# A build-time order planner: a shared port for VectorE and GpSimd, and a lower planned cost for running sums

## The chip, the cores and the metric

The kernel runs on one core of a Trainium2 chip. Its time is the device time of one execution in microseconds (us); a lower one is better. Five engines matter: TensorE (PE in the profile; its weight loads are PEld), VectorE (DVE), ScalarE (ACT), GpSimd (POOL) and SyncE (SP), which issues the DMAs.

## The reference

Two layers (`DEPTH` 2) work on 512 latent tokens and 256 context tokens of width 1024. A layer normalizes and modulates its input, projects it once, runs three mixers beside each other, multiplies each by a gate, merges them and adds the result to the residual. The last layer computes outputs for the latent tokens alone.

```python
shift, scale, gate = jnp.split(sc @ w_mod + b_mod, 3, axis=-1)
h = rms_norm(x, norm_g) * (1 + scale[:, None]) + shift[:, None]
aq, ak, av, az, bq, bk, bv, bo, bz, bg, cq, ck, cv, cz, gm = split_proj(h @ w_in)
...
y_a = diff_head_norm(o_a, da_g, lam_init) * jax.nn.silu(az)
...
y_b = mlstm_out(h_b, bo, bz, ml_g)
...
y_c = o_c.reshape(B, S, BR_W) * jax.nn.silu(cz)

x = x + gate[:, None] * merge_branches((y_a, y_b, y_c), gm, w_br, w_out)
```

A is differential attention (two softmaxes per head, the second subtracted), B a bidirectional linear recurrence whose decays come from the gate columns `bg`, and C neighbourhood attention (32 columns of keys around each block of 16 query columns, and the context).

## The kernel before, in words

**The work of TensorE.** Its main stream is one long list of projections: for each of branch C, A and B the values (`proj_v`), keys, queries and gates of two heads or pairs at a time, then the merge gates and the branch projections (`wbr`), then the output projection (`wout`). All these matmuls write tiles named `pj`, of which two exist. Weights come by DMA in half tiles `wr`; ScalarE rounds each to its high half and GpSimd subtracts that from the original for the low half, both into a tile `wh`, of which four exist (`Stream.lower`; 409 of the 416 low halves are GpSimd's). Three matmuls multiply high by high, high by low and low by high.

**Side tasks** fill in between: for branch C scores `gp<-qk`, a row minimum (`m`), a biased copy with minimum (`p<-gp,cb,m`), exponentials, a normalization (`smc`, `p<-p,smc`), transposes `gp<-ident,p`, their copies `pt`, and the product with the values `gp<-pt,cb` and `gp<-pt,v`; for A the same in a single score tile `sc`, with minima `mna`; for B products with running sums. Three tasks have a fixed place: the **gates chain** (`branch_b_gates`), some twenty VectorE steps over 112 x 768 elements in one `v` and one `pt` tile, ending in copies `pt<-v` and twelve column transposes `gp<-ident,pt`; **`norm_rows`**, which transposes sums of squares (`gp<-ident,p`), takes the inverse root on 128 x 2 or 128 x 4 elements (`rr`, `rt`), and spreads it by `gp<-p,ones`; and **`make_h`**, which makes the projection's input `h` from it, two VectorE instructions and one of ScalarE for each of eight tiles and each segment (latents, context). In the merge of layer 0 `mod_rows` computes the rest of the modulation: 112 sums over 128 x 512 elements on VectorE, two inputs in SBUF (`cb`), the products dumped into the PSUM tile `sc`.

**What sets the order.** Nothing is reordered on the chip: a planner, `Sched`, runs while the program is built. `Timed` gives each instruction a cost from its size, and `run` adds it to the planned clock of its engine, `T`, not before the planned ends of what it reads and writes (`ready`). Each side task is a generator with its own planned time; between main matmuls, `slot` lets those run whose planned time has come. So a cost decides where an instruction stands in its engine's queue, and the chip then executes each queue in that order. `need` holds the main stream until a buffer is planned to be free, and the order of the side tasks goes on meanwhile: there are two `v` tiles, so the next `proj_v` needs the one that the gates chain holds, until that chain's last copies.

```python
    def need(self, tag):
        while not self._take(tag, self.T["P"]):
            self.idle()
```

Every recorded compute instruction carries the line of `Timed`'s last call, L344 before, so the names of the tiles tell groups apart; matmuls are L379 (`mm`), transposes L383 (`tr`), DMAs L331.

Of the kernel before, what the change touches and what calls it, by code (L numbers as in the profile page):

```python
# [19 lines left out]
PSUM = bass.MemoryType.PSUM  # L20
DRAM = bass.MemoryType.DRAM

D = 1024
# [64 lines left out]
class Chain:  # L88


    def __init__(self, gen, t, eng="P"):
        self.gen, self.t, self.eng, self.want, self.landed = gen, t, eng, None, 0.0
# [13 lines left out]
class Sched:  # L106
# [14 lines left out]
    def __init__(self, free):  # L121
        self.free = {t: [0.0] * n for t, n in free.items()}
        self.token = {}
        self.T = dict(P=0.0, D=0.0, A=0.0, G=0.0, S=0.0, Q=0.0, H=0.0)
        self.main = self.cur = Chain(None, 0.0)
        self.high, self.mid, self.side, self.hooks = [], [], [], []
        self.pe = 0.0
        self.seen = {}

    @staticmethod  # L130
    def span(ap):
# [31 lines left out]
    def run(self, eng, cost, reads, writes):  # L163
        c = self.cur
        start = max(self.T[eng], self.ready(eng, reads, writes))
        end = self.T[eng] = start + cost
        self.note(eng, reads, writes, end)
        c.settle()
        c.t, c.eng = end, eng
        if eng == "P" and c is not self.main:  # L170
            self.pe += cost
# [125 lines left out]
def _space(ap):  # L297
    return getattr(ap, "space", None)


def _elems(ap):
    n = 1
    for s in list(ap.shape)[1:]:
        n *= int(s)
    return n


class Timed:
# [5 lines left out]
    def __getattr__(self, name):  # L314
        f = getattr(self.real, name)

        def call(*args, **kw):
            aps = [v for v in list(args) + list(kw.values()) if hasattr(v, "shape")]
            n = max(_elems(v) for v in aps)
            small = sum(1 for v in aps if _elems(v) == 1 and n > 1)  # L320
            psum = any(_space(v) == PSUM for v in aps[1:] + aps[:1])
            writes = [kw["out"] if "out" in kw else args[0]]
            if "accum_out" in kw:
                writes.append(kw["accum_out"])
            if name == "tensor_tensor_reduce":
                writes.append(args[-1])
            reads = [v for v in aps if not any(v is w for w in writes)]
            if name == "dma_start":
                out = kw["out"]
                self.sched.dma(int(out.shape[0]), int(out.shape[0]) * _elems(out) * 4, reads, writes)  # L330
                return f(*args, **kw)  # L331
            if self.eng == "D":
                one = len([v for v in aps if _elems(v) == n]) <= 2 and name in ("tensor_copy", "tensor_scalar", "memset")
                cost = n / (1.92 if one and not psum else 0.96) + 69.0 + 61.0 * small
                if name == "reciprocal":
                    cost = 69.0 + 8.0 * n
                if name == "tensor_tensor_reduce":
                    cost += 220.0
            elif self.eng == "A":
                cost = n * 0.8333 + (51.0 if psum else 93.0) + 93.0 * small  # L340
            else:
                cost = n * 2.15 + 130.0
            self.sched.run(self.eng, cost, reads, writes)
            return f(*args, **kw)  # L344
        return call
# [1594 lines left out]
```

## Time and profile before

| what | value |
|---|---|
| time, median of 3 runs | 1974.73 us (1974.41 to 1976.49) |
| profiled execution: time | 1975.63 us |
| profiled execution: span | 1973.9 us |
| mean granted clock of TensorE | 0.984 |
| PE busy | 1865.8 us (95%) |
| DVE busy | 1363.2 us (69%) |
| ACT busy | 862.1 us (44%) |
| POOL busy | 617.3 us (31%) |

The span runs from the first to the last recorded instruction; the execution's time lies 1.7 us above it. "Idle before" a group is time in which its engine waited, with the engine and tile that released it. [...] Busy times of VectorE and GpSimd hold whatever an instruction waits for after it began.

### The profile page before, as it was taken

Reading aid. Unit: us, or ns where it says so; the run is one execution under the profiler, and the core shown is the slowest. Engines: PE = TensorE matmul, PEld = TensorE weight load, DVE = VectorE, ACT = ScalarE, POOL = GpSimd, SP = SyncE. Lnnn points to the kernel's source line nnn. Section 1 sums busy time; section 2 is a strip of 40 time slices with the busy share of each in tenths; the row PEclk is TensorE's granted clock in tenths of the full one; section 3 lists DMA queues with packets and bytes.
Section 4 is the critical chain, followed back from the end, with each engine's and each line's share of the span. In section 5 each row is a group of like instructions: output and inputs, shape, how many; then the busy total and the mean of one; then the engine's idle time right before and its main releaser. Section 6 shows DMA issues by size and latency. Waiting matters only on the chain.

```text
span 1973.9 us, 31993 instructions
## 1 busy us (share of the span) xinstructions
PE 1865.8 (95%) x11420; PEld 1636.1 (83%) x11420; DVE 1363.2 (69%) x3165; ACT 862.1 (44%) x1972; POOL 617.3 (31%) x498
## 2 busy tenths in 40 slices
PE   5989999999999999999999898999999999999997
PEld 2879998988889888888887777898979787888886
DVE  6587775888787877687835768676887777743336
ACT  4345544555544553222223444555555444433343
POOL 1242322121222222333334533424222323334454
PEclk9989999999999999999999999999999999999998
DMA  8233323222211122566645423333231212335554
GB/s 316 72 96 102 96 79 97 61 82 65 68 51 51 44 83 76 182 227 200 214 152 169 147 78 111 119 94 109 69 105 54 65 50 69 97 109 186 168 167 124
DMA packets 137247, 222.26 MB, mean 113 GB/s; under 512 B 15984, under 2 KB 47776, under 8 KB 137088
## 3 DMA queue, kind: packets, MB, share of 16 engines
q1 hardware_dynamic: 137088, 220.22, 35.6%
q8 instruction: 91, 1.49, 0.3%
q14 instruction: 68, 0.56, 0.1%
HBM read 177.36 MB, written 28.11 MB: 104 GB/s over the span
## 4 chain that ended last, share of the span: by engine, by line
PE 47%; issue 21%; DVE 17%; POOL 9%; ACT 3%; DMA 2%; SPq 0%; POOLq 0%; DVEq 0%; ACTq 0%
PE pj L379 34%; POOL wh L344 8%; PE gp L379 7%; PE gp L383 3%; DVE p L344 3%; PE sc L379 3%; DVE qk L344 2%; DVE pt L344 2%; DVE t L344 1%; DMA cb<-in_wmodr_dram 1%; DVE v L344 1%; DVE sc L344 1%; ACT wh L344 1%; DVE h L344 1%; ACT p L344 1%
## 5 line engine op out<-in xcount | busy, mean ns | idle before, releaser
L379 PE MATMUL pj<-h,wh 128*128 128x512 f32 (+1 forms) x5664 | 1124.4, 351 | 20.1 <-DVE gz L344 9.9
L379 PEld LDWEIGHTS pj<-h,wh 128*128 128x128 f32 x5664 | 897.3, 191 | 144.0 <-DVE gz L344 10.3
L344 POOL TENSOR_TENSOR wh<-wr,wh 128x512 fp32r<-128x512 f32 x409 | 558.9, 1372 | 1269.4 <-ACT wh L344 1250.8
L344 ACT CAST wh<-wr 128x512 fp32r<-128x512 f32 x416 | 256.9, 620 | 395.5 <-PE pj L379 193.4
L379 PE MATMUL pj<-wh,h 128*128 128x256 f32 x1728 | 239.3, 289 | 4.1 <-DVE h L344 2.5
L379 PEld LDWEIGHTS pj<-wh,h 128*128 128x128 f32 x1728 | 219.7, 193 | 7.1 <-DVE h L344 3.7
L344 DVE TENSOR_TENSOR pt<-gp,pt 128x512 fp32r<-128x512 f32 (+1 forms) x224 | 123.6, 572 | 80.2 <-ACT pt L344 79.2
L344 ACT CAST pt<-gp 128x512 fp32r<-128x512 f32 (+1 forms) x224 | 105.1, 497 | 155.6 <-PE gp L383 155.1
L379 PE MATMUL pj<-v,wh 128*128 128x512 f32 (+1 forms) x576 | 161.6, 357 | 6.5 <-DVE t L344 6.2
L383 PE MATMUL gp<-ident,p 128*128 128x128 f32 x720 | 110.3, 278 | 23.4 <-DVE p L344 15.5
L379 PEld LDWEIGHTS pj<-v,wh 128*128 128x128 f32 x576 | 103.5, 189 | 23.9 <-DVE t L344 7.9
L379 PE MATMUL gp<-pt,v 128*128 128x256 f32 x864 | 120.2, 287 | 0.0
L383 PEld LDWEIGHTS gp<-ident,p 128*128 128x128 f32 x720 | 84.0, 142 | 40.4 <-issue 18.1
L379 PEld LDWEIGHTS gp<-pt,v 128*128 128x128 f32 x864 | 113.0, 195 | 2.0
L344 ACT ACTIVATE t<-pj 128x512 f32<-128x512 f32 (+1 forms) x118 | 63.4, 538 | 99.7 <-PE pj L379 93.5
L379 PE MATMUL pj<-qk,wh 128*128 128x512 f32 (+1 forms) x288 | 102.2, 355 | 0.0
L344 DVE TENSOR_REDUCE mna<-sc 128x1 f32<-128x768 f32 (+1 forms) x80 | 67.8, 847 | 38.5 <-PE sc L379 38.3
L344 DVE SCALAR_TENSOR_TENSOR t<-t,pj 128x512 f32<-128x512 f32 x66 | 38.8, 594 | 73.2 <-PE pj L379 71.2
L344 ACT ACTIVATE p<-sc,mna 128x768 f32<-128x768 f32 (+1 forms) x80 | 65.5, 819 | 53.7 <-DVE mna L344 53.5
L379 PE MATMUL sc<-qk 128*128 128x512 f32 (+1 forms) x360 | 82.0, 336 | 5.0 <-ACT p L344 4.9
L344 DVE CUSTOM_DVE_ANT_0 sc<-cb,prm 128x512 f32<-128x512 f32 x56 | 60.0, 1072 | 25.4 <-DMA cb<-in_wmodr_dram 24.1
L344 DVE TENSOR_TENSOR qk<-t,qk 64x768 fp32r<-64x768 f32 (+1 forms) x64 | 64.0, 1000 | 14.2 <-ACT qk L344 11.8
(157 smaller groups left out, 2208.8 us busy)
## 6 DMA issues: line engine op xcount, KB each, us to landing
wr<-in_wu_dram SPq DMA_DIRECT2D x304, 256.0 KB, 2.9
cb<-in_wmodr_dram SPq DMA_DIRECT2D x64, 256.0 KB, 3.4
wr<-in_wout_dram SPq DMA_DIRECT2D x64, 256.0 KB, 2.8
wr<-in_wbr_dram SPq DMA_DIRECT2D x48, 256.0 KB, 2.9
q<-qk SPq DMA_DIRECT2D x160, 64.0 KB, 2.4
cb<-vd SPq DMA_DIRECT2D x32, 256.0 KB, 3.2
qk<-in_xT_dram SPq DMA_DIRECT2D x16, 384.0 KB, 5.0
pd<-t SPq DMA_DIRECT2D x16, 384.0 KB, 3.9
```

Of the source, the lines that this page charges most:

```text
L344: return f(*args, **kw)
L379: PE.matmul(o, l, r, start=start, stop=stop)
L383: PE.transpose(o, i, idn)
```

## The change

`Sched` remembers the last eight planned intervals of GpSimd and of those VectorE instructions that neither read nor write PSUM. A GpSimd instruction, or such a VectorE instruction, whose planned start falls into an interval of the other engine is planned to start at that interval's end. Besides, the planned cost of `tensor_tensor_reduce` (the running sums and minima) loses the 220 ns that were added to its length. Nothing else changes: every engine gets the same instructions, the same number of each, in another order. The lines of the later file lie nine further down (L353, L388, L392).

```diff
@@ -126,6 +126,15 @@
         self.high, self.mid, self.side, self.hooks = [], [], [], []
         self.pe = 0.0
         self.seen = {}
+        self.port = {"D": deque(maxlen=8), "G": deque(maxlen=8)}
+
+    def shared(self, eng, start, cost):
+
+        for a, b in self.port["G" if eng == "D" else "D"]:
+            if a <= start < b:
+                start = b
+        self.port[eng].append((start, start + cost))
+        return start
 
     @staticmethod
     def span(ap):
@@ -163,6 +172,8 @@
     def run(self, eng, cost, reads, writes):
         c = self.cur
         start = max(self.T[eng], self.ready(eng, reads, writes))
+        if eng == "G" or eng == "D" and not any(_space(v) == PSUM for v in list(reads) + list(writes)):
+            start = self.shared(eng, start, cost)
         end = self.T[eng] = start + cost
         self.note(eng, reads, writes, end)
         c.settle()
@@ -334,8 +345,6 @@
                 cost = n / (1.92 if one and not psum else 0.96) + 69.0 + 61.0 * small
                 if name == "reciprocal":
                     cost = 69.0 + 8.0 * n
-                if name == "tensor_tensor_reduce":
-                    cost += 220.0
             elif self.eng == "A":
                 cost = n * 0.8333 + (51.0 if psum else 93.0) + 93.0 * small
             else:
```

Three places where the order moved. First TensorE in branch C of layer 0, where the gates chain's twelve column transposes `gp<-ident,pt` stand among the main stream (`pj`). Before:

```order
L379 MATMUL pj<-h,wh 128x256 x24
L383 MATMUL gp<-ident,pt 128x112 x2
L379 MATMUL pj<-h,wh 128x512 x3
L383 MATMUL gp<-ident,pt 128x112 x2
L379 MATMUL pj<-h,wh 128x512 x3
L383 MATMUL gp<-ident,pt 128x112 x8
```
After:

```order
L388 MATMUL pj<-h,wh 128x512 x24
L388 MATMUL gp<-pt,cb 128x256 x6
L388 MATMUL gp<-pt,v 128x256 x6
L388 MATMUL pj<-h,wh 128x256 x6
L392 MATMUL gp<-ident,p 128x128 x8
L388 MATMUL pj<-h,wh 128x256 x18
L388 MATMUL pj<-wh,h 128x256 x6
L392 MATMUL gp<-ident,pt 128x112 x2
L388 MATMUL pj<-wh,h 128x256 x6
L392 MATMUL gp<-ident,pt 128x112 x4
L388 MATMUL pj<-wh,h 128x256 x6
L392 MATMUL gp<-ident,pt 128x112 x6
```
Before, the first two transposes stand right ahead of the gate projection's 24 matmuls of 512 columns and the other ten among these. After, the first two follow all 24 of them, the 24 of 256 columns behind these (6 and 18) and six matmuls of the next `proj_v` (`pj<-wh,h`).

Second, TensorE in branch C of layer 1, from the last gate projection of the first pairs (`pj<-h,wh`) on; `proj_v` of the other pairs is `pj<-wh,h`, and it needs the `v` tile that the gates chain holds. Before:

```order
L379 MATMUL gp<-qk 128x256 x2
L379 MATMUL gp<-qk,q_12892 128x256 x2
L379 MATMUL pj<-wh,h 128x256 x6
L383 MATMUL gp<-ident,pt 128x112 x4
L379 MATMUL pj<-wh,h 128x256 x6
L383 MATMUL gp<-ident,pt 128x112 x2
L379 MATMUL pj<-wh,h 128x256 x18
L383 MATMUL gp<-ident,pt 128x112 x2
L379 MATMUL pj<-wh,h 128x256 x12
L383 MATMUL gp<-ident,pt 128x112 x4
L379 MATMUL gp<-qk 128x256 x2
L379 MATMUL gp<-qk,q_12944 128x256 x2
```
After:

```order
L388 MATMUL pj<-h,wh 128x512 x3
L388 MATMUL gp<-qk 128x256 x2
L388 MATMUL gp<-qk,q_12908 128x256 x2
L388 MATMUL gp<-qk 128x256 x2
L388 MATMUL gp<-qk,q_12954 128x256 x2
L388 MATMUL gp<-pt,cb 128x256 x6
L388 MATMUL gp<-pt,v 128x256 x6
L392 MATMUL gp<-ident,p 128x128 x8
L388 MATMUL gp<-qk 128x256 x2
L388 MATMUL gp<-qk,q_12954 128x256 x2
L388 MATMUL gp<-qk 128x256 x2
L388 MATMUL gp<-qk,q_13068 128x256 x2
```
Before, the next `proj_v` follows the score groups of one block and goes on between transposes. After, no main matmul stands in the 28 rows that begin with the second one here: four rounds of two score groups, `gp<-pt,cb`, `gp<-pt,v` and eight transposes, before `pj<-wh,h` begins.

At the same place VectorE, the rows that end in the gates chain's last copies, `pt<-v` of 64 partitions. Before:

```order
L344 TENSOR_TENSOR pt<-gp,pt 128x4x128
L344 TENSOR_TENSOR smc<-smc 128x1
L344 RECIPROCAL smc<-smc 128x1
L344 TENSOR_SCALAR p<-p,smc 128x512
L344 TENSOR_TENSOR qk<-t,qk 64x512
L344 COPY pt<-v 64x512
L344 COPY pt<-v 64x256
L344 COPY pt<-v 64x512
L344 COPY pt<-v 64x256
```
After:

```order
L353 COPY pt<-v 48x768 x2
L353 TENSOR_TENSOR pt<-gp,pt 128x4x128
L353 TENSOR_TENSOR smc<-smc 128x1
L353 RECIPROCAL smc<-smc 128x1
L353 TENSOR_SCALAR p<-p,smc 128x512
L353 TENSOR_REDUCE m_13293<-gp 128x1
L353 ISA p,m_13296<-gp,cb,m_13293 128x256
L353 ISA m_13296 128x1
L353 COPY pt<-v 64x512
L353 COPY pt<-v 64x256
L353 COPY pt<-v 64x512
L353 COPY pt<-v 64x256
```
Between the first gate product `gz<-gz,pj` there (which moved ahead of four instructions of the gates chain) and these copies stand, before, 5 minima `m` with their biased copies, 3 normalizations (the rows `smc`, `smc`, `p<-p,smc`) and 1 copy `pt<-gp,pt`; after, 12, 10 and 8 of them, one more `gz<-gz,pj`, and six strided products `gz<-gp,gz`.

Third, TensorE at the boundary of the layers: the output projection of the context (`pj<-h,wh`, 192 matmuls of 256 columns), `norm_rows` of the latents (`gp<-ident,p` x4 and `gp<-p,ones`), and the first `proj_v` of layer 1 (`pj<-wh,h`). Before:

```order
L379 MATMUL pj<-h,wh 128x256 x36
L383 MATMUL gp<-ident,p 128x128 x4
L379 MATMUL pj<-h,wh 128x256 x54
L379 MATMUL gp<-p,ones 128x512
L379 MATMUL pj<-h,wh 128x256 x102
L379 MATMUL pj<-wh,h 128x256 x30
```
After:

```order
L388 MATMUL pj<-h,wh 128x256 x42
L392 MATMUL gp<-ident,p 128x128 x4
L388 MATMUL pj<-h,wh 128x256 x150
L392 MATMUL gp<-ident,p 128x128 x2
L388 MATMUL gp<-p,ones 128x512
L388 MATMUL pj<-wh,h 128x256 x42
```
The spreading matmul `gp<-p,ones`, on which all of `make_h` waits, stood after 90 of the 192 and stands after the last; 30 matmuls of `proj_v` became 42 up to the next side row.

## Rows read from the trace of the kernel before

**Rows 1.** The page: busy time of each engine, share of the span, instructions.
```profile
PE 1865.8 (95%) x11420; PEld 1636.1 (83%) x11420; DVE 1363.2 (69%) x3165; ACT 862.1 (44%) x1972; POOL 617.3 (31%) x498
```
**Rows 2.** PE's waits by releaser: us in total, times, longest.
```profile
PE gp L383 <- DVE p L344: 15.5, 17, 3.0
...
PE pj L379 <- DVE t L344: 8.9, 10, 1.2
```
**Rows 3.** Timeline near the end, POOL and DVE: start, us, instruction, [idle before].
```profile
1937.56 4.15 POOL L344 TENSOR_TENSOR wh<-wr,wh 128x512 fp32r<-128x512 f32 x3 [0.90 <-ACT wh L344]
...
1938.90 0.16 DVE L344 SCALAR_TENSOR_TENSOR rr<-rt,rr 128x2 f32<-128x2 f32 x1
1939.10 1.20 DVE L344 TENSOR_TENSOR rt<-rr 128x2 f32<-128x2 f32 x1
```
**Rows 4.** The tile sc on DVE: duration ns min/median/max, first and last start.
```profile
L344 DVE CUSTOM_DVE_ANT_0 sc<-cb,prm x56: 747/760/1893, 805.0 to 1004.2; 128x512 f32<-128x512 f32 x56
```
**Rows 5.** The page: the same group, busy and mean ns.
```profile
L344 DVE CUSTOM_DVE_ANT_0 sc<-cb,prm 128x512 f32<-128x512 f32 x56 | 60.0, 1072 | 25.4 <-DMA cb<-in_wmodr_dram 24.1
```
**Rows 6.** Timeline of DVE and POOL in the merge of layer 0.
```profile
886.67 1.54 POOL L344 TENSOR_TENSOR wh<-wr,wh 128x512 fp32r<-128x512 f32 x1 [0.15 <-ACT wh L344]
...
887.16 1.60 DVE L344 CUSTOM_DVE_ANT_0 sc<-cb,prm 128x512 f32<-128x512 f32 x1
```
**Rows 7.** Timeline of PE at three waits.
```profile
102.97 4.90 PE L379 MATMUL pj<-h,wh 128*128 128x512 f32 x12 [4.87 <-DVE gz L344]
...
128.35 0.64 PE L383 MATMUL gp<-ident,pt 112*128 112x112 f32 x2 [3.09 <-DVE pt L344]
...
1641.63 0.52 PE L383 MATMUL gp<-ident,p 128*128 128x128 f32 x3 [1.74 <-DVE ht L344]
```
**Rows 8.** Windows: us, busy of each engine (x), PEclk, DMA share, GB/s.
```profile
128.40:134.40 6.00, 6.00 (x24) 5.21 (x25) 3.95 (x28) 0.00 (x0) 0.43 (x1) 0.50 0.54 155
...
1643.00:1646.50 3.50, 3.50 (x13) 2.81 (x12) 1.51 (x3) 0.75 (x2) 0.00 (x0) 0.51 0.10 33
...
1188.50:1192.50 4.00, 3.95 (x18) 3.96 (x19) 3.93 (x4) 0.09 (x1) 0.00 (x0) 0.50 0.07 18
```
**Rows 9.** Timeline of PE in the gate stage of layer 1.
```profile
1188.55 1.65 PE L379 MATMUL pj<-h,wh 128*128 128x256 f32 x6 [3.52 <-DVE gz L344]
...
1212.34 0.88 PE L379 MATMUL pj<-wh,h 128*128 128x256 f32 x6
```
**Rows 10.** DVE by form, 1176 to 1253 us: busy us, mean ns, idle before.
```profile
L344 DVE TENSOR_TENSOR pt<-gp,pt 128x512 fp32r<-128x512 f32 x11 | 7.4, 688 | 3.6 <-ACT pt L344 3.5
L344 DVE TENSOR_SCALAR p<-p,smc 128x512 f32<-128x512 f32 x12 | 7.2, 601 | 0.4
L344 DVE CUSTOM_DVE_ANT_0 p<-gp,cb,m 128x256 f32<-128x256 f32 x14 | 6.8, 484 | 1.9
L344 DVE TENSOR_REDUCE m<-gp 128x1 f32<-128x256 f32 x14 | 5.9, 418 | 0.1
L344 DVE TENSOR_TENSOR smc<-smc 128x1 f32<-128x1 f32 x12 | 4.5, 375 | 0.1
```
**Rows 11.** Timeline between the layers, PE and DVE.
```profile
1106.49 2.38 PE L379 MATMUL pj<-h,wh 128*128 128x256 f32 x18 [1.38 <-DVE rr L344]
...
1133.38 6.00 PE L379 MATMUL pj<-wh,h 128*128 128x256 f32 x48
...
1119.05 0.74 DVE L344 SCALAR_TENSOR_TENSOR h<-qk,modc,h 128x512 fp32r<-128x512 f32 x1
```
**Rows 12.** Timeline near the end, PE and DVE.
```profile
1943.15 1.01 PE L379 MATMUL gp<-p,ones 128*128 128x256 f32 x2 [2.06 <-DVE p L344]
...
1944.20 2.05 DVE L344 SCALAR_TENSOR_TENSOR qk<-qk,prm,gp 128x256 f32<-128x256 f32 x5 [0.59 <-PE gp L379]
```
**Rows 13.** The page: the two steps after a score group of branch A.
```profile
L344 DVE TENSOR_REDUCE mna<-sc 128x1 f32<-128x768 f32 (+1 forms) x80 | 67.8, 847 | 38.5 <-PE sc L379 38.3
...
L344 ACT ACTIVATE p<-sc,mna 128x768 f32<-128x768 f32 (+1 forms) x80 | 65.5, 819 | 53.7 <-DVE mna L344 53.5
```

## The prediction

> **What bounds the kernel now.** I read the page first: PE is busy for 95% of the span and VectorE for 69% [rows 1]. So PE's main stream sets the time, and only two things can move it: idle time of PE, and stretches at its lower clock. The view of PE's waits comes next. Apart from two DMA waits of the first 14 us, nearly all of it is owed to VectorE: normalized rows `p` for transposes 15.5 us in 17 waits, evacuations `t` 8.9 us in 10 [rows 2]. GpSimd releases no wait of PE. In the timeline the single waits are seen: 4.87 us at 102.97 for a gate product, 3.09 at 128.35 for the gates chain's `pt`, 1.74 at 1641.63 for an inverse root [rows 7]. [...]
>
> Last I read why VectorE is late. At 1938.90 a step on 128x2 elements takes 0.16 us, the next one, of the same size, 1.20 us; GpSimd works without a break from 1937.56 to 1941.71 [rows 3]. Such pairs are all over the trace: the additions on 128x1 elements in layer 1's gate stage have a mean of 0.375 us [rows 10]. The planner of before does not know this, so it puts PE's transposes too early behind VectorE's chains.
>
> **The change, part by part.** No instruction is added or removed; all counts stay. Everything is a question of where side rows stand, so each term is a wait taken away or made.
>
> *Running sums.* 112 sums of `mod_rows` were planned at 0.944 us and are planned at 0.724 (512 elements at 0.96 per ns, 69, and 61 for each of two scalars). The median of those shown is 0.760, the lowest 0.747 [rows 4]: the new length is that of an undisturbed one. Their mean is 1.072 [rows 5], though, because some meet GpSimd: 1.60 us at 887.16, with GpSimd busy from 886.67 to 888.21 [rows 6]. The new rule never sees that, since these sums dump into PSUM and are exempt. [...]
> The sums lie in the merge of layer 0, between evacuations `t` for which PE waited 10 times, 8.9 us. They now bunch more tightly: up to 14 between two evacuations instead of 12. Two more at 1.072 are 2.1 us in the worst bunch, if PE waits there at all. Bounds 0 and 6 (0.6 for each of the ten waits); I take a **loss of 2**.
>
> *Later consumers.* I looked for every side row of PE that waited over 0.3 us (56.9 us in all after 90 us) in the new order. 28.5 us of these belong to rows that now stand later, in main matmuls, by at least their wait; 11 of it at the places treated below. The other 17.5 are spread over all branches, 3.1 at 128.35 and 1.7 at 1641.63 the largest [rows 7]. What they wait for moved too, and some rows (a wait of 3.0 us for `p`, the longest of its group [rows 2]) moved forward instead. Bounds 6 and 17.5; I take two thirds, a **gain of 12**.
>
> *The lower clock behind them.* 128.40 to 134.40 costs 3.0 us (half of 6.0), 1643.00 to 1646.50 1.7 [rows 8]. With the waits gone these go. Bounds 0 and 4.7; a **gain of 4**. Two gate products in layer 0 and near the end add little: the one of 102.97 is one gates-chain step earlier on VectorE, **gain 1** (0 to 4.9).
>
> *The gate stage of layer 1 (second place).* Before, the next `proj_v` begins at 1212.34 [rows 9]. After, PE first has 28 side rows, which end with transposes of the tenth normalization, shortly ahead of the last copies `pt<-v`. Up to those copies VectorE has 7 minima with their biased copies more (0.418 + 0.484, 6.3 us), 7 normalizations (0.375, 0.601 and a reciprocal like the small steps of 0.16 [rows 3], 8.0 us), 7 copies `pt` (0.688, 4.8 us) [rows 10], and, by my estimate from these, 2 to 3 us of gate products: about 22 us. The first gate product is some 7 us earlier, since four gates-chain steps now follow it. VectorE has nothing to give: in 1188.50 to 1192.50 it is busy 3.93 of 4.00 us [rows 8]. So main restarts 15 us later, near 1227; if the port costs as before, 1232. The 3.52 us wait at 1188.55 [rows 9] goes, and counts for nothing, as VectorE sets the restart. In exchange PE has by then done 12.3 us of side work (28 rows, 13.1 us at 0.12 us for 256 columns, less what of it was done by then before) that it did later. That leaves 3 to 8 us, and 2 to 3 for a stretch at the lower clock, which PE falls to when it waits like this (0.50 at 1188.50). Bounds 0 and 15; a **loss of 8**. Behind the held main stream wait the weights' pipeline and all later projections.
>
> *The boundary of the layers (third place).* Before, at 1106.49, 120 of the 192 matmuls of `wout` are left [rows 11]; at 0.125 us (6.00 for 48 [rows 11]) and without today's waits they end near 1121.5. Only then `gp<-p,ones` runs, and behind it VectorE makes eight tiles `h`, two instructions of 0.74 us each [rows 11]: 11.8 us, to 1133.5, and with the hand-overs and evacuations in between 1135 to 1137. Before, `proj_v` ran free at 1133.38, with 30 of its matmuls done. Loss 2 to 4, and up to 3 for the lower clock behind an idle stretch of 12 us. Bounds 0 and 9; a **loss of 4**.
>
> *Scores of branch A.* There is one tile `sc`: after a group, a minimum of 0.847 us and an exponential of 0.819 us [rows 13] must end before the next may be written, with hand-overs 2.3 us for 768 columns, 1.5 for 256. Adding up the matmuls between groups in the new order (0.23 us for 512 columns, between half of the 0.41 of those at 102.97, which ran at the lower clock [rows 7], and twice the 0.125), eight groups stand too near, by 8.6 us in all; before three, by 1.4. Bounds 0 and 8; a **loss of 5**.
>
> *The end.* `gp<-p,ones` of the first half, which waited 2.06 us at 1943.15, stands 144 matmuls later; five output products that took 2.05 us [rows 12] now come in front of the last half's sums. **Gain 1**, bounds -1 and 3.
>
> *Weights.* Low halves on GpSimd are planned later too, up to the end of a VectorE interval. I cost that at nothing: the cover is the four `wh` tiles, GpSimd keeps its 409 halves in the same sequence, is busy 31% [rows 1], and no PE wait of before is owed to it. If the cover failed, one half costs about 1.4 us of main stream.
>
> **Sum.** Gains 12 + 4 + 1 + 1 = 18; losses 2 + 8 + 4 + 5 = 19. The profiled execution took 1975.6 us, so it would take 1976.6; the median of the runs is 0.9 below that execution, hence **1975.7 us**, no change that can be told (0.2%, about what a measurement of this kernel tells from none, is 3.9 us).
>
> **Rivals.**
> *The gain prevails.* An order that follows the port leaves VectorE ahead of PE nearly everywhere; then the consumers' gain is its bound (5.5 more), the scores are not late (3 less), the boundary costs 2 (2 less) and the block in layer 1 is paid by its side work (5 less): 15.5 us, **1960** at its fullest and 1966 without the 5.5. For it: most of PE's waits are VectorE's chains. Against it: both large losses stand in the order itself.
> *The main stream is held in layer 1's gate stage.* If VectorE is still blocked there as before (0.375 us for 128x1), the main stream starts at 1233 or later, and if the side work done ahead is worth half, since VectorE is behind and the next transposes wait as well, the loss is 20 instead of 8: **1988**. It decides from about 1228 on; earlier than that, the other terms do.
> *The change does not do what it says.* The sums are the operations it shortens, and they still meet GpSimd: with 0.4 to 0.6 us at each of ten evacuations, 6 instead of 2, and no gain by the lower length: **1979.7**. [...]
>
> **Chances.** Cancelling gains and losses 0.40, own range 1968 to 1983 (0.10 of it faster by over 0.2%, 0.22 within, 0.08 slower); the gain prevails 0.28; the held main stream 0.24; blind sums 0.08 (0.03 within, 0.05 slower). Faster 0.38, same 0.25, slower 0.37. The range leaves out a tenth on each side: below 1960 all gains would be at their bound, above 1990 two losses. All bounds together reach from about 1945 to 2008.
>
> **What would show it.** Right: the rows at 128 and 1641 without their waits and at full clock; `sc` waits for `p` that grow by some 5 us; PE idle before `pj<-wh,h` in layer 1's gate stage, with VectorE busy throughout, and its start 13 to 20 us after 1212 less what was gained before; `pj<-wh,h` waiting for `h` between the layers. Wrong: new waits at the rows that moved forward; VectorE's busy time falling by tens of us, so that both blocks cost nothing; waits for `wh`.

## The result and the profile after

The changed kernel takes 1986.54 us (median; 1985.25 to 1990.37), the kernel before 1974.57 us (1972.71 to 1976.49): a ratio of 1.0064, 95% interval 1.0046 to 1.0082. It is slower by 0.6%. The forecast was no change (1975.7), with an own range of 1968 to 1983. The measured time lies outside that, inside the whole range of 1960 to 1990, near the 1988 of the rival to which the prediction gave 0.24. The profiled execution took 1987.83 us at a span of 1985.8, so 11.9 us of span are to be found.

The page after, engines first, then the granted clock in 40 slices:

```profile
PE 1876.1 (94%) x11420; PEld 1645.7 (83%) x11420; DVE 1330.9 (67%) x3165; ACT 866.6 (44%) x1972; POOL 616.3 (31%) x498
...
PEclk9999999999999999999999897999999999999998
```

Against [rows 1], VectorE is busy 32.3 us less, with small steps and sums that are shorter in the mean (`hs<-ht,hs` on 128x2 elements 0.198 us instead of 0.271, `sc<-cb,prm` 0.963 instead of 1.072, with 23 of its 56 overlapping a GpSimd instruction instead of 28): on the whole the two engines do meet less, as planned. Yet PE, with the same instructions, is busy 10.3 us more, and that is most of the 11.9: it ran longer at a granted clock of 0.50 (the mean is 0.976 instead of 0.984), above all in the slices around 1130 and 1220 us. PE's waits after, by releaser (us in total, times, longest):

```profile
PE sc L388 <- ACT p L353: 16.9, 10, 4.1
PE gp L392 <- DVE p L353: 15.5, 14, 3.1
...
PE pj L388 <- DVE t L353: 11.0, 16, 1.7
PE pj L388 <- ACT h L353: 5.9, 3, 3.4
...
PE pj L388 <- DVE gz L353: 3.8, 2, 3.5
```

The largest group of before is as large as it was [rows 2]. The main stream's waits for gate products fell from 10.7 to 3.8 us (those of the transposes `gp` for them rose from 0.2 to 3.5); waits for the one score tile rose from 4.9 to 16.9.

Where the time went is seen best when each matmul of PE's main stream is set against the same matmul of before. The table gives that difference at ten places, by their time before (negative: ahead of before), for this kernel and the experiments below. Each row is one execution: at 90 us, ahead of all branches, the rows differ from before by -0.5 to 2.7 us already, and the 19 executions of before that were taken beside e17, e19 and e20 spread from 1969.21 to 1978.91. So a difference of 1 or 2 us in the table shows nothing by itself.

| kernel | 273 | 357 | 446 | 778 | 1094 | 1168 | 1292 | 1535 | 1782 | 1955 |
|---|---|---|---|---|---|---|---|---|---|---|
| changed kernel | -11.8 | -14.9 | 0.2 | -1.1 | 2.1 | 8.8 | 16.2 | 27.4 | 13.3 | 10.1 |
| e1 port alone | -11.2 | -5.3 | -5.8 | -5.8 | -5.9 | 0.8 | 6.0 | 21.4 | 19.1 | 15.7 |
| e2 length alone | -14.2 | -7.9 | -9.5 | -11.9 | -4.4 | -4.4 | -1.4 | 2.0 | 0.0 | 1.0 |
| e3 | -11.3 | -14.3 | 0.0 | -1.7 | 1.9 | 1.9 | 9.0 | 20.0 | 5.9 | 5.2 |
| e4 | -12.6 | -15.6 | -1.3 | -2.9 | -0.2 | 6.8 | 8.2 | 19.7 | 5.6 | 2.1 |
| e5 | -12.2 | -15.2 | -0.2 | -1.8 | 2.0 | 1.9 | 2.6 | 14.3 | 0.0 | -3.4 |
| e14 | -15.3 | -9.0 | -10.6 | -12.9 | -9.4 | -9.4 | -6.5 | -2.6 | -4.7 | -6.0 |
| e17 | -15.8 | -9.5 | -11.1 | -13.8 | -12.8 | -7.2 | 0.3 | 11.4 | -2.9 | -6.0 |
| e18 | -15.2 | -8.8 | -10.4 | -13.1 | -13.8 | -12.5 | -9.6 | -5.9 | -7.6 | -6.5 |
| e20 | -15.3 | -9.0 | -10.7 | -13.3 | -14.7 | -13.2 | -13.3 | -12.9 | -12.6 | -13.9 |
| e22 | -15.7 | -9.4 | -11.0 | -13.6 | -1.1 | -1.2 | -1.2 | -1.2 | -0.3 | -0.6 |

Inside a stage the figure also holds side work that is done sooner or later. At 1094 (behind the merge of layer 0), 1168, 1292 and 1782 (merge of layer 1) as many side matmuls lie behind as in before. At 778 (end of the branches of layer 0) the changed kernel has 31 of them still to do, 3.2 us by my estimate at 0.12 us for 256 columns (e3, e4 and e5 the same, e1 29), while e2 and the rows from e14 on are 10 or 12 ahead, about 1 us. So the changed kernel leaves the branches of layer 0 2.1 us behind before, not 1.1 ahead. It loses nothing in the merge, where PE waits 8.8 us for evacuations, as against 8.9, then 6.7 at the boundary of the layers and 7.4 in the gate stage, and gets 2.9 back by 1782 and 1.4 up to the end.

**The boundary.** PE after (start, us, instruction, [idle before]):

```profile
1103.25 18.48 PE L388 MATMUL pj<-h,wh 128*128 128x256 f32 x150
1124.80 0.41 PE L392 MATMUL gp<-ident,p 128*128 128x128 f32 x2 [3.07 <-DVE p L353]
1125.49 2.00 PE L388 MATMUL gp<-p,ones 128*128 128x512 f32 x2 [0.28 <-DVE p L353]
1130.89 0.58 PE L388 MATMUL pj<-wh,h 128*128 128x256 f32 x1 [3.40 <-ACT h L353]
1132.77 2.78 PE L388 MATMUL pj<-wh,h 128*128 128x256 f32 x11 [1.30 <-DVE h L353]
...
1138.06 5.79 PE L388 MATMUL pj<-wh,h 128*128 128x256 f32 x29 [1.30 <-DVE h L353]
```

The 150 matmuls run through without a wait, ending at 1121.7 as worked out, but the spreading matmul starts 4 us later still. VectorE shows why. Before, the inverse root of the latents took from 1100.84 to 1110.37, diagonals (`p<-ident,rr`) included, with two evacuations among its steps; its first and last row:

```profile
1100.84 0.69 DVE L344 TENSOR_REDUCE ms<-gp 128x4 f32<-128x512 f32 x1 [0.42 <-PE gp L383]
...
1107.56 2.81 DVE L344 TENSOR_SCALAR p<-ident,rr 128x128 f32<-128x128 f32 x4
```

After, an evacuation, two steps of the inverse root, and its last row:

```profile
1108.13 1.30 DVE L353 TENSOR_TENSOR p<-p,t 128x256 f32<-128x256 f32 x1 [1.84 <-ACT t L353]
...
1109.75 0.85 DVE L353 SCALAR_TENSOR_TENSOR rr<-rt,rr 128x4 f32<-128x4 f32 x1
...
1112.23 0.15 DVE L353 TENSOR_TENSOR rt<-rr 128x4 f32<-128x4 f32 x1
...
1124.57 0.87 DVE L353 TENSOR_SCALAR p<-ident,rr 128x128 f32<-128x128 f32 x4
```

By the new rule a step is planned behind an interval of GpSimd, and in the order evacuations of the context stand between the steps. On the chip the queue is kept: the step of 0.15 us at 1112.23, whose input `rr` was done at 1110.60, comes behind two evacuations (1110.53 and 1111.01). Others of these wait for ScalarE (1.84 us at 1108.13) and PE (0.83 us at 1116.01) themselves, and the chain takes from 1103.53 to 1125.4. The turns that were planned don't hold there either: five steps of the chain still take 0.85 to 1.25 us, while GpSimd works on low halves nearly without a break (from 1104.98 to 1123.76 it is busy 16.85 of 18.78 us).

**The gate stage.** PE after, and then windows as in [rows 8]: one where before had half clock (0.50), two in branch A of layer 0, one at the boundary, one here, and another where before had half clock:

```profile
1213.40 0.50 PE L388 MATMUL gp<-qk 128*128 128x256 f32 x2 [3.33 <-DVE pt L353]
...
1219.58 0.63 PE L392 MATMUL gp<-ident,p 128*128 128x128 f32 x4 [1.34 <-DVE gz L353]
...
1237.65 0.63 PE L392 MATMUL gp<-ident,p 128*128 128x128 f32 x4 [2.17 <-DVE gz L353]
...
1245.09 1.69 PE L388 MATMUL pj<-wh,h 128*128 128x256 f32 x12
```

```profile
128.40:134.40 6.00, 6.00 (x40) 5.46 (x39) 5.74 (x14) 1.77 (x6) 0.81 (x2) 1.00 0.68 192
374.70:381.50 6.80, 6.08 (x19) 5.12 (x20) 3.70 (x14) 1.99 (x6) 0.00 (x0) 0.50 0.06 21
422.50:429.30 6.80, 6.21 (x20) 5.08 (x21) 4.17 (x12) 2.44 (x7) 0.00 (x0) 0.50 0.06 15
1125.60:1142.60 17.00, 10.37 (x36) 7.92 (x37) 14.29 (x33) 5.76 (x9) 0.00 (x0) 0.50 0.15 36
1214.30:1245.00 30.70, 22.79 (x103) 20.35 (x104) 28.28 (x76) 11.84 (x39) 6.29 (x8) 0.61 0.25 70
1643.00:1646.50 3.50, 3.50 (x17) 2.87 (x17) 3.14 (x7) 2.18 (x5) 1.40 (x2) 1.00 0.25 75
```

The main stream restarts at 1245.09, where [rows 9] had 1212.34, and PE works from 1214 to 1245 at a mean clock of 0.61, with VectorE busy 28.28 of 30.70 us. At 128 and 1643 the half clock is gone (1.00 in both windows), as forecast.

**Branch A of layer 0** is where the forecast had near score groups, but no held main stream. PE after:

```profile
371.34 0.39 PE L388 MATMUL sc<-qk 128*128 128x256 f32 x1 [1.75 <-ACT p L353]
...
375.42 1.54 PE L392 MATMUL gp<-ident,p 128*128 128x128 f32 x6 [2.14 <-DVE p L353]
...
416.11 0.39 PE L388 MATMUL sc<-qk 128*128 128x256 f32 x1 [1.22 <-ACT p L353]
...
421.51 0.61 PE L388 MATMUL sc<-qk 128*128 128x512 f32 x2 [1.85 <-ACT p L353]
```

In the order the main stream is held here too, behind 5.1 us of side rows from 416.11 on: three score groups, which share one tile, stand in them with little between, and two wait for the exponential of the one before, 1.22 and 1.85 us. The lead of 14.9 us at 357 is gone at 446: by the estimate above 5 us of that are side matmuls that were put off at 357 (4.0) and are ahead at 446 (1.1), and 10 are lost.

### The profile page after: what moved, and what is told of

Same layout as the page of the kernel before. It is cut to its first block, busy times and chain, and to the rows that moved or that the text cites. A ratio compares the mean times of both kernels' runs of the same rounds, so it can differ in the third digit from the quotient of the medians.

```text
span 1985.8 us, 31973 instructions
## 1 busy us (share of the span) xinstructions
PE 1876.1 (94%) x11420; PEld 1645.7 (83%) x11420; DVE 1330.9 (67%) x3165; ACT 866.6 (44%) x1972; POOL 616.3 (31%) x498
## 5 line engine op out<-in xcount | busy, mean ns | idle before, releaser
L388 PE MATMUL pj<-h,wh 128*128 128x512 f32 (+1 forms) x5664 | 1118.5, 350 | 14.7 <-DVE t L353 5.0
L388 PEld LDWEIGHTS pj<-h,wh 128*128 128x128 f32 x5664 | 896.7, 191 | 140.5 <-issue 7.1
L353 POOL TENSOR_TENSOR wh<-wr,wh 128x512 fp32r<-128x512 f32 x409 | 557.5, 1370 | 1280.9 <-ACT wh L353 1261.6
L353 ACT CAST wh<-wr 128x512 fp32r<-128x512 f32 x416 | 256.8, 620 | 408.6 <-PE pj L388 220.9
L388 PE MATMUL pj<-wh,h 128*128 128x256 f32 x1728 | 242.9, 292 | 7.9 <-ACT h L353 4.0
L388 PEld LDWEIGHTS pj<-wh,h 128*128 128x128 f32 x1728 | 223.6, 196 | 12.2 <-ACT h L353 5.9
L353 DVE TENSOR_TENSOR pt<-gp,pt 128x512 fp32r<-128x512 f32 (+1 forms) x224 | 123.5, 571 | 88.5 <-ACT pt L353 87.3
L353 ACT CAST pt<-gp 128x512 fp32r<-128x512 f32 (+1 forms) x224 | 105.5, 497 | 170.4 <-PE gp L392 169.9
L388 PE MATMUL pj<-v,wh 128*128 128x512 f32 (+1 forms) x576 | 163.2, 358 | 6.0 <-DVE t L353 6.0
L392 PE MATMUL gp<-ident,p 128*128 128x128 f32 x720 | 111.8, 280 | 23.5 <-DVE p L353 15.5
L388 PE MATMUL gp<-pt,v 128*128 128x256 f32 x864 | 123.2, 291 | 0.7 <-DVE pt L353 0.6
L388 PEld LDWEIGHTS pj<-v,wh 128*128 128x128 f32 x576 | 103.4, 189 | 22.8 <-DVE t L353 7.9
L392 PEld LDWEIGHTS gp<-ident,p 128*128 128x128 f32 x720 | 85.9, 144 | 40.2 <-issue 13.2
L388 PEld LDWEIGHTS gp<-pt,v 128*128 128x128 f32 x864 | 115.1, 199 | 3.1 <-DVE pt L353 1.0
L353 ACT ACTIVATE t<-pj 128x512 f32<-128x512 f32 (+1 forms) x118 | 63.4, 537 | 110.9 <-PE pj L388 110.6
L388 PE MATMUL pj<-qk,wh 128*128 128x512 f32 (+1 forms) x288 | 102.2, 355 | 0.0
L353 DVE TENSOR_REDUCE mna<-sc 128x1 f32<-128x768 f32 (+1 forms) x80 | 67.7, 847 | 50.2 <-PE sc L388 49.9
L388 PE MATMUL sc<-qk 128*128 128x512 f32 (+1 forms) x360 | 83.4, 340 | 16.9 <-ACT p L353 16.9
L353 DVE SCALAR_TENSOR_TENSOR t<-t,pj 128x512 f32<-128x512 f32 x66 | 38.6, 593 | 73.3 <-PE pj L388 73.3
L353 ACT ACTIVATE p<-sc,mna 128x768 f32<-128x768 f32 (+1 forms) x80 | 65.6, 820 | 48.4 <-DVE mna L353 47.8
L388 PEld LDWEIGHTS sc<-qk 128*128 128x128 f32 x360 | 59.6, 191 | 28.0 <-ACT p L353 20.7
L353 DVE TENSOR_TENSOR qk<-t,qk 64x768 fp32r<-64x768 f32 (+1 forms) x64 | 67.2, 1049 | 23.0 <-ACT qk L353 21.5
```

Source lines behind the costliest of these rows:

```text
L388: PE.matmul(o, l, r, start=start, stop=stop)
L392: PE.transpose(o, i, idn)
```

## The experiments

All ratios are to the kernel before, on the same chip.

**Each edit alone** (e1, e2): in e1 the 220 ns are put back, in e2 they are removed from the kernel before.

```diff
                 if name == "tensor_tensor_reduce":
                     cost += 220.0
```

> The shared port alone; running sums keep their 220 ns. Theory P (the port rule makes the loss, since it postpones only VectorE instructions with both ends in SBUF, so the long single chains fall behind and TensorE is held for what they release): as slow as the changed kernel or more, 1982 to 1992 us, because in this order too the main stream waits behind 10.7 us of side rows in the gate stage of layer 1, and the spreading matmul stands behind all of the output projection. Rival S (the shorter sums make the loss, by bunching): no slower than before, 1971 to 1978 us.

> The 220 ns of the running sums removed, no shared port. Theory P: no loss, 1968 to 1977 us; no score group of branch A stands too near in this order (0 us short against 1.4 before and 8.6 after), the main stream is nowhere held, and the boundary of the layers is as before. Rival S: 1983 to 1989 us. If the sums of the merge suffer from being planned too short (the term of 2 us), it is 2 us over before.

Measured: e1 1.0106 (1.0074 to 1.0137), e2 1.0002 (0.9987 to 1.0017). e1, at 1995.27 us, is slower than even theory P had it. The port rule makes the whole loss and more; with it in place, the shorter sums take about 0.4% off, though the intervals of e1 and of the changed kernel overlap. Rival S falls.

**The port rule suspended at a place** (e3, e4, e5, e17, e18). A switch stands ahead of the rule, and is set in the layer's code:

```diff
-        if eng == "G" or eng == "D" and not any(_space(v) == PSUM for v in list(reads) + list(writes)):
+        if self.turns and (eng == "G" or eng == "D" and not any(_space(v) == PSUM for v in list(reads) + list(writes))):
```

```diff
+        if l == 0:
+            mg = merge()
+            S_.turns = False
+            return finish(*mg)
...
                 vt, vflag = proj_v("cv", g, None if g else hook)
+                if l == 1 and g == 0:
+                    S_.turns = True
```

That is e3; e4 sets `S_.turns = g == 1` for layer 1 behind that `proj_v`, e5 is the first part of e3 and turns the rule on at `g == 1`.

> The changed kernel without the shared port from the output projection of layer 0 to the end of the first values of layer 1: there the spreading matmul stands after 90 of 192 matmuls again, as before; the rest of the order stays that of the changed kernel. Theory B (the boundary costs 6 to 7 us for good, half of it at the lower clock): 1978 to 1982 us, the stretch of 17 us at half clock from 1125 gone. Rival C (what is lost there is given back later, as VectorE gets ahead): 1984 to 1988 us.

> The changed kernel without the shared port between the first and the second values of layer 1, the gate stage: no block of side rows over 4 us is left there. Theory G (the held main stream costs 7 to 8 us net, after the side work done ahead is credited): 1977 to 1981 us, and the half clock from 1214 to 1245 mostly gone. Rival C (the side work done ahead pays for it): 1984 to 1988 us.

> The changed kernel without the shared port from the output projection of layer 0 to the second values of layer 1, so both places at once. If the two losses are separate (0.25% and 0.31% less than the changed kernel when one is undone), this is 11 us faster than the changed kernel, 1973 to 1977 us, within 0.2% of before. If they are one and the same delay (VectorE late at the boundary makes the gate stage late), undoing both gives no more than one, 1979 to 1982 us.

Measured: e3 1.0039 (1.0025 to 1.0054), e4 1.0033 (1.0018 to 1.0049), e5 1.0004 (0.9992 to 1.0016). Of the 0.64% these are 0.25%, 0.31% and 0.60%: 4.9, 6.1 and 11.8 us, each with an uncertainty of 4 to 5 us by the intervals. The two losses add up, so they are separate; rival C falls. In e3's PE rows the spreading matmul is back ahead of half of the output projection, with the wait of before:

```profile
1112.37 1.10 PE L389 MATMUL gp<-p,ones 128*128 128x512 f32 x2 [1.62 <-DVE p L354]
1112.90 7.02 PE L389 MATMUL pj<-h,wh 128*128 128x256 f32 x54
...
1134.10 1.23 PE L389 MATMUL pj<-wh,h 128*128 128x256 f32 x8 [0.40 <-DVE h L354]
```

In e4's the main stream goes on at 1220.22, and the columns of the gates chain follow it. The lower clock was expected mostly gone and isn't: 17.1 us at 0.50 or 0.51 lie between 1192 and 1230, in three stretches.

```profile
1220.22 0.87 PE L389 MATMUL pj<-wh,h 128*128 128x256 f32 x6
1220.94 0.55 PE L393 MATMUL gp<-ident,pt 112*128 112x112 f32 x4
```

The remaining question was why a kernel that is planned with truer sums only equals before. e17 turns the rule on at the merge of layer 0 (`S_.turns = True` ahead of `finish(*merge())`), so that only the branches of layer 0 lose it.

> The changed kernel with the shared port only from the merge of layer 0 on, so that branches C, A and B of layer 0 are ordered by the shorter sums alone. Theory L (in the changed kernel the shared port costs these branches 10 to 13 us: with the sums alone the main stream leaves them 12 us ahead of before, with the port 0 to 3 behind): 1972 to 1977 us, the two stretches of half clock at 374 and 422 gone. Rival (the lead would be lost at the two later places anyway): 1981 to 1988 us.

Measured: 0.9999 (0.9988 to 1.0011), 0.65% below the changed kernel. In the table it is 13.8 us ahead at 778, as e2 is with 11.9, the changed kernel 1.1; at 1094, free of side work, e17 is 12.8 ahead and the changed kernel 2.1 behind. PE's waits from 300 to 480 us, of the changed kernel and of e2:

```profile
PE sc L388 <- ACT p L353: 8.9, 4, 4.1
PE gp L392 <- DVE p L353: 3.7, 3, 2.1
```

```profile
PE gp L381 <- DVE p L342: 2.4, 3, 1.4
PE sc L377 <- ACT p L342: 1.4, 2, 0.9
```

So beside the shorter sums the port rule has three losses, about 13, 5 and 6 us, and the sums one gain, 12 us in the same branches of layer 0, which the first loss hides. The first of these does not stand for the rule alone: in e1, without the shorter sums, layer 0 ends 5.9 us ahead of before (1094). Each edit by itself gains there, and both together lose. e1 loses 6.7 and 5.2 us at the two places like the changed kernel, and 13.1 more between 1292 and 1782; its order has two more blocks of side rows there, of 6.0 us at 1446 and 7.9 at 1647 by the estimate of 0.12 us for 256 columns. That these make that loss is not shown.

**One direction** (e9): in `shared`, `start = b if eng == "G" else start`.

> The changed kernel with the shared port in one direction: GpSimd is planned to wait for VectorE, VectorE no longer for GpSimd. Theory P (it is the postponed VectorE chains that do the harm): like the shorter sums alone, 1971 to 1979 us, the main stream nowhere held and 90 matmuls before the spreading one. Rival W (the low halves of the weights, planned later, hold the main stream): 1982 us or more.

Measured: 1.0008 (0.9998 to 1.0019), like the shorter sums alone. The low halves of the weights, planned later, cost nothing that can be told; what costs is VectorE's part of the rule, its postponed instructions. Rival W falls.

**The merge** (e14, e18). e2 loses 7.5 us of its lead between 778 and 1094. e14 keeps the 220 ns where the first operand is in PSUM (`and _space(args[0]) == PSUM`); e18 takes e2 and turns the port rule on in the merge of layer 0 alone.

> No shared port; the 220 ns removed from the sums of branches B and C, but kept for the 112 sums of the merge that dump into PSUM. Theory M (with the shorter sums alone the layers' first branches gain 13 us and the merge gives 8 to 9 of it back, since its sums, really 0.93 to 1.0 us long, are planned at 0.72 and bunch ahead of evacuations): 1963 to 1969 us, faster than both kernels, the main stream 12 us ahead of before at the end of the merge. Rival (the merge loses through something else, such as where its loads land): 1972 to 1977 us, as with the shorter sums everywhere.

> The shorter sums everywhere, the shared port only in the merge of layer 0. In the changed kernel the merge lost nothing, with the shorter sums alone 8 us. If the shared port is what spaces the evacuations there: 1963 to 1969 us. If not: 1972 to 1977 us.

Measured: e14 0.9977 (0.9967 to 0.9987), e18 0.9983 (0.9971 to 0.9994): both faster than either kernel, neither by as much as expected. In the merge e18 does what was expected and keeps all of its lead; e14 keeps 9.4 of 12.9 us, where 12 were expected. The rest goes in layer 1, where both drop 6 to 7 us from 1168 to 1535, as e2 does. In the merge e2 also has 10.3 us at the lower clock (880.5 to 887.3 and 938.5 to 942.0), e18 none. The waits of PE from 780 to 1060, of e2, then of e14:

```profile
PE pj L377 <- DVE t L342: 12.4, 11, 4.0
```

```profile
PE pj L379 <- DVE t L344: 10.9, 11, 2.5
```

**What these point to** (e19, e20): the shorter sums in layer 0 alone, by a flag set with `S_.long = l == 1` ahead of the branches; e19 with the long sums in the merge and no port rule, e20 with e18's merge. The edit shown is e20's.

```diff
+                if name == "tensor_tensor_reduce" and self.sched.long:
+                    cost += 220.0
```

> No shared port; the sums of branches B and C of layer 0 planned without the 220 ns, those of the merge and of layer 1 with them. Theory (the shorter length helps layer 0 by 12 to 13 us and costs layer 1 some 6): 1962 to 1968 us. Rival (the gain in layer 0 is passed on in part only, whatever the sums of layer 1): 1969 to 1972 us, as with the length removed in both.

> As the run before, but with the shorter sums and the shared port in the merge of layer 0 instead of the long sums there. If the merge keeps the whole lead, as it did with the shared port in the merge alone: 1960 to 1966 us, 2 to 4 below the run before. If not, the same as that.

Measured: e19 0.9954 (0.9939 to 0.9969), 1966.46 us; e20 0.9935 (0.9917 to 0.9952), 1961.18 us. e20 beats both kernels, and in the table it holds its lead of 13 us from 778 to the end. That it is faster than e19 is not shown (the intervals overlap). The window from 110 to 780 us, of e20 and then of the changed kernel:

```profile
110.00:780.00 670.00, 659.10 (x4420) 594.16 (x4419) 506.64 (x1410) 338.41 (x867) 160.63 (x137) 1.00 0.25 77
```

```profile
110.00:780.00 670.00, 649.05 (x4318) 587.88 (x4318) 487.80 (x1362) 335.29 (x852) 157.15 (x137) 0.98 0.25 74
```

In the same time e20 has done 102 more recorded matmuls, without a stretch at the lower clock, although VectorE is busy 18.8 us longer.

**The sums that dump into PSUM** (e22): e20, but in the merge VectorE instructions with two inputs in SBUF take turns as well.

```diff
-... eng == "D" and not any(_space(v) == PSUM for v in list(reads) + list(writes)) ...
+... eng == "D" and (sum(_space(v) != PSUM for v in reads) > 1 or not any(_space(v) == PSUM for v in list(reads) + list(writes))) ...
```

> As the run with the shared port in the merge of layer 0 and the shorter sums in layer 0, but in that merge VectorE instructions with two inputs in SBUF take turns as well, so the 112 sums that dump into PSUM are no longer exempt. Rival of the prediction (the change is blind where it shortens, at 0.4 to 0.6 us for each of ten evacuations): 4 us faster than that run, 1955 to 1959 us. Theory (the merge waits for its evacuations by 0.7 us each whatever the planner believes of the sums): within 2 us of it, 1959 to 1964 us.

Measured: 0.9985 (0.9972 to 0.9997), 1972.45 us: neither of the two expectations. By the ratios it is 10 us slower than e20, all of it in the merge (from 13.6 us ahead to 1.1), where PE waits for evacuations 18.0 us in 13 waits; the first row is e22's, the second e20's, 780 to 1060 us:

```profile
PE pj L391 <- DVE t L356: 18.0, 13, 3.1
```

```profile
PE pj L391 <- DVE t L356: 8.8, 13, 1.3
```

The sums don't meet GpSimd less often for it: the two groups of 56 have means of 0.994 and 0.942 us in e22, 0.958 and 0.980 in e20, and 28 sums take over 1 us in either. So e22 shows what this rule does to the order; what those meetings cost, it can't show.

## Why the prediction failed in its forecast, and where it was right

*What bounds the kernel* held in the main: the difference is made of PE's waits and of the lower clock behind them (0.50 from 1125.60, say, behind the wait of 3.07 us at 1124.80), and VectorE's busy time, down by 32.3 us, did not count. But "nearly all" of the waits being VectorE's was misread: of 84 us of PE's waits for engines before, 18.4 were for ScalarE, and the group that grew most, by 12.0 us, waits for ScalarE's exponentials.

*The gate stage*, a loss of 8, measured 7.4 in the table and 6.1 by e4. The main stream restarted later than the 1232 given as a bound, at 1245.09, of which 8.8 us came in with the stream itself; that is 24 us of its own instead of 15 to 20, against which 17 came back by 1292, instead of 12. Both parts were too small by about the same, so that the sum fits is partly luck. *The boundary*, a loss of 4, measured 6.7 and 4.9 by e3. Its matmuls ended when they were said to; what was mis-sized is the start of `gp<-p,ones`, which was to run right then. The forecast took for granted that the inverse root would be ready, and the order had queued its steps behind evacuations; and the lower clock, put at up to 3 us, held for 17.0 us in which PE was busy 10.37. *The end* was a gain of 1 and measured 1.4; the waits at 1943 are gone.

The step that failed is *later consumers*, the gain of 12 with the 4 of the *lower clock behind them*. The forecast matched rows that waited with where they now stand, and took two thirds of their waits as won. The rows at 128 and 1643 did lose their waits and their half clock. But with the *scores of branch A* taken at a loss of 5, the branches of both layers should have given about 12 us net, and gave about 1: a loss of 2.1 in layer 0 and a gain of 2.9 in layer 1. The total of 56.9 us from which the term starts isn't borne out either: in the view of PE's waits, those of side rows after 90 us add up to 49.5. In layer 0 e17 shows what took the gain: beside the shorter sums the port rule costs these branches about 13 us, most of it between 357 and 446, where 10 us are lost. The rule alone, in e1, did gain there, 5.9 us up to 1094. Waits for the score tile grew by 12.0 us instead of 5, and two stretches of half clock, from 374.7 and 422.5 on, replaced the two that went, from 127.5 and 260.6 on, each 6.8 us. I had measured how near score groups stand, and had seen one place where the main stream is held; the order has two more, 5.1 us of side rows in branch A of layer 0 and 4.4 in layer 1 (from 1501 on), which the same reading would have shown.

*Running sums*: a loss of 2 was forecast, and the merge lost nothing in the changed kernel: side by side with the port rule, bunching did no harm there. For the rest of the edit the forecast had no term: alone, the shorter length is worth 12 us in the branches of layer 0, gives 7.5 back in the merge and the rest in layer 1 (e2). The gain in layer 0 is less idle time of PE and the clock, from 110 to 780 us of before and of e2:

```profile
110.00:780.00 670.00, 650.77 (x4339) 590.63 (x4339) 506.79 (x1388) 334.78 (x859) 154.77 (x136) 0.98 0.25 74
```

```profile
110.00:780.00 670.00, 658.11 (x4416) 592.73 (x4415) 511.98 (x1412) 338.35 (x868) 160.44 (x137) 1.00 0.27 78
```

How the shorter length brings this is not shown row by row.

*Weights* at nothing was right (e9). Of the rivals, the held main stream came nearest, with 1988, and that is coincidence. One half of its condition occurred, a main stream that starts at 1233 or later (1245.09); the other, work done ahead that is worth half, did not (17 of 24 us came back). Its place lost 6 to 7 us and not 20, and two other places made up the sum. The rival of blind sums is right in its premise: the sums do still meet GpSimd (mean 0.963 and 0.938 us in the changed kernel, the longest 1.883, where the 72 of the 112 that overlap no GpSimd instruction take 0.746 to 0.761, and the other 40 have a mean of 1.296). In its consequence it is refuted: the merge lost nothing, and the shorter length did gain (e2). Planning turns for these sums too, in e22, made the merge over 10 us slower and took none of the meetings away. Why stays open.

## What to carry to other kernels

A planner's cost that is nearer to the truth isn't yet a better order: a chain whose steps are postponed one by one gets other work between them, and the queue keeps it there (the inverse root at the boundary took 21.9 us instead of 9.5). Before trusting such a change, read in the new order where the main stream stands behind side rows, and how far the row that releases a whole stage has moved; both could be read here without running anything. Try a planning rule stage by stage and each edit by itself: the same rule cost 13 us in one stage beside another edit, gained there without it, and in another stage was part of the fastest version.

## What was not expected of the hardware

The granted clock of TensorE stayed at 0.50 for all of 1125.60 to 1142.60, 17.0 us in which it was busy 10.37 us, while its waits went on. The two waits ahead of it in the stage are of 3.07 and 0.28 us, and the longest within it is of 3.40. Of the 11.9 us of added span only 1.6 are added idle time of PE (108.1 us before, 109.7 after); the rest is the same instructions, busy for longer at a mean granted clock of 0.976 instead of 0.984.
